# Six per-token inverse roots: spread over the partitions by way of a row in DRAM instead of by TensorE, and the attention pairs of the second layer in another order

## The chip, the core and the metric

The kernel runs on one core of one Trainium2 chip. The core's TensorE (PE, with its weight loads PEld), VectorE (DVE), ScalarE (ACT) and GpSimd (POOL) run their own instruction streams, each in program order; SyncE (SP) here only issues DMAs. The metric is the device time of one execution in microseconds (us): 894.42, the median of three runs (894.36 to 894.44). Lower is better.

## The reference, cut to what matters

```
h = rms_norm(x)                       # n1: 512 tokens x 1024 features
q, k, v, z_a, b, c, u, z_c = h @ w_in
attn = softmax_1(q k) - lam * softmax_2(q k)   # 4 heads, two score maps each
attn = rms_norm(attn @ v) * silu(z_a)          # "an": one norm per head
x = x + rms_norm([attn, conv] @ w_out)         # n2
x = x + sigmoid(x @ w_gate) * rms_norm(p @ w_ple)   # n3
y = gmlp(rms_norm(x))                 # n4; a_w_in -> u, v, z; a_w_out
x = x + rms_norm(y)                   # n5
k, v = rms_norm(x) @ w_kv             # shared by all heads of the next layer
x = x + rms_norm(swa(rms_norm(x), k, v))   # n6; b_w_in, 16 heads, window 128; b_w_out
```

Every `rms_norm` needs, for each token, 1/sqrt(mean of squares + eps).

## The kernel before, in words

Activations lie feature-major: 128 features on the partitions, the 512 tokens along the free axis. All products are float32 made of parts: a tensor is split into a rounded high part (`whi`, `h1h`; ACT copies) and the rest (`wlo`, `h1l`; DVE subtractions), and three matmuls (high x high, high x low, low x high) make one product. Weights arrive as `raw` (128 x 1024, 512 KB) by DMAs of SP, each waiting for its buffer; ACT makes `whi`, DVE makes `wlo`, and the wlo is the last reader of the raw.

The reciprocal roots come out of `cols` as `rstd` with the tokens on the partitions (128 x 4: four blocks of 128 tokens). A feature-major tensor needs the same 512 numbers as a row on every partition. Five kinds of norms (`WIDE` at L42: an, n1, n3, n4, n6) do this in `bcast_wide` (L434): DVE splits rstd into `rh` and `rl`, POOL multiplies each with the identity (`dgh`, `dgl`, 128 x 512), PE multiplies these with a matrix of ones (two matmuls into `bc`), and for an, n1 and n4 ACT copies PSUM to SBUF (`n1rb`, `anrb`, `n4rb`). n1's row is first used by the evictions of q (`ev<-w_in,n1rb`), a head's row by `at<-pv,gsub,anrb` (L207), n4's row by the evictions of u and z, which come after the columns of v (those use n4's columns, not its row).

The order of the program is made when it is built, by a planner (`Flow`, L86 to L150). It holds a model clock for each engine and for each tensor a time at which it is ready; stages are generators that `yield` what they wait for, or a number of model nanoseconds, and the one that is ready first is written next. A change of one model time therefore moves instructions on every engine. On the chip each engine then runs its stream in that order and waits by semaphores.

The second layer's attention takes its work in pairs (pr, b): pr is one half of the heads, b a block of 128 tokens; `ORDER_B` (L38) is their order, `PACE_B` the model time between two units. A pair gives scores `bsc`, transposed probabilities `btr`, `bph`/`bpl`, products `bpv`, the output `y`, its parts `ybh` and `ybl`, and these go into `b_w_out`. `h_tokens` transposes the residual (`ht`, eight groups of four transposes), started at H_START and spaced by PACE_H.

Of the kernel before, what the change touches and what calls it, by code (L numbers as in the profile page):

```python
# [10 lines left out]
F32 = mybir.dt.float32  # L11
F32R = mybir.dt.float32r
AF = mybir.ActivationFunctionType
# [4 lines left out]
P = 128  # L18
T = 512
NT = T // P  # L20
# [14 lines left out]
HB_AT = 7  # L35
POOL_ST6 = False
DENSE_B = (0, 1, 2, 3, 4, 5, 6, 7, 8, 9, 10, 11, 12, 13, 14, 15)
ORDER_B = tuple((pr, b) for pr in range(2) for b in range(4))  # L38
AHEAD_END = 1
H_START = 8000  # L40
LAM_AT = 40000
WIDE = ('an', 'n1', 'n3', 'n4', 'n6')  # L42
LAT = 130.0
KLATE = 3
BANKS = 7

PACE_A, PACE_B, PACE_LN, PACE_H = 4500, 3500, 8000, 4000
WARM = 10


# [35 lines left out]
class Flow:  # L86
# [14 lines left out]
    def at(self, aps):  # L101
        return max((self.ready.get(a.tensor.name, 0.0) + LAT for a in aps), default=0.0)

# [50 lines left out]
def block(ctx: ExitStack, tc: tile.TileContext, xT, pT, w_in, w_out, w_ple, w_gate, a_w_in, a_w_out,  # L154
          w_kv, b_w_in, b_w_out, vecs, rows, bs_rows, gp_rows, csts, w_sT, tri, tabA, tabB, out):
    nc = tc.nc
# [3 lines left out]
    ring = ctx.enter_context(tc.tile_pool(name="ring", bufs=RING))  # L160
    wraw = ctx.enter_context(tc.tile_pool(name="wraw", bufs=WRAW))
    whl = ctx.enter_context(tc.tile_pool(name="whl", bufs=WHL))
    small = ctx.enter_context(tc.tile_pool(name="small", bufs=6))
    psum = ctx.enter_context(tc.tile_pool(name="psum", bufs=8, space=PSUM))
    F = Flow()
    uid = [0]

    def nm(s):
        uid[0] += 1
        return f"{s}_{uid[0]}"  # L170

    def rt(name, dt=F32):
        return ring.tile([P, T], dt, tag="r", name=nm(name))

    def rt2(name):
        return rt(name + "h", F32R), rt(name + "l", F32R)
# [5 lines left out]
    def pst(name):  # L182
        live[0] += name in COUNTED
        return psum.tile([P, T], F32, tag="ps", name=nm(name))
# [10 lines left out]
    def size(a):  # L195
        return math.prod(a.shape[1:])

    def is_ap(*args):
        return [a for a in args if not isinstance(a, (int, float, type(None)))]

    def act(o, a, func, bias=0.0, scale=1.0, accum_out=None, after=0.0):
        nc.scalar.activation(o, a, func, bias=bias, scale=scale, accum_out=accum_out)  # L202
        ex = is_ap(bias, scale, accum_out)
        F.op("act", 80 + 0.84 * size(o) + 93 * len(ex), [o] + is_ap(accum_out), [a] + is_ap(bias, scale), after)

    def stt(o, a, sc, b, op0, op1):
        nc.vector.scalar_tensor_tensor(o, a, sc, b, op0, op1)  # L207
        F.op("dve", 70 + 1.04 * size(o) + 65 * len(is_ap(sc)), [o], [a, b] + is_ap(sc))

    def tt(o, a, b, op, after=0.0):  # L210
        nc.vector.tensor_tensor(o, a, b, op)  # L211
        F.op("dve", 70 + 1.04 * size(o), [o], [a, b], after)

    def ptt(o, a, b, op):
        nc.gpsimd.tensor_tensor(o, a, b, op)  # L215
        F.op("pool", 350 + 260 * size(o) if op == ALU.pow else 100 + 2.4 * size(o), [o], [a, b])
# [17 lines left out]
    def vcopy(o, a):  # L234
        nc.vector.tensor_copy(o, a)
        F.op("dve", 70 + 0.8 * size(o), [o], [a])
# [6 lines left out]
    def mm(o, a, b, start, stop, cost=None):  # L243
        nc.tensor.matmul(o, a, b, start=start, stop=stop)  # L244
        F.op("pe", cost or max(107.0, 2 + b.shape[-1] / 2.4), [o], [a, b])

    def mm3(o, a, b, first, last):
        (ah, al), (bh, bl) = a, b
        mm(o, ah, bh, first, False)
        mm(o, ah, bl, False, False)  # L250
        mm(o, al, bh, False, last)
# [176 lines left out]
    def bcast(r, half=None):  # L428

        o = pst("bc")  # L430
        for t in range(NT) if half is None else (2 * half, 2 * half + 1):
            mm(o[:, t * P:(t + 1) * P], r[:, t:t + 1].to_broadcast([P, P]), ident, True, True, 224)
        return o

    def bcast_wide(r, out):

        rh = small.tile([P, NT], F32R, tag="rh", name=nm("rh"), bufs=2)
        rl = small.tile([P, NT], F32R, tag="rl", name=nm("rl"), bufs=2)
        vcopy(rh, r)
        tt(rl, r, rh.bitcast(F32), ALU.subtract)  # L440
        ds = rt2("dg")
        for d, h in zip(ds, (rh, rl)):
            v = d.rearrange("p (t c) -> p t c", c=P)
            ptt(v, ident.unsqueeze(1).to_broadcast([P, NT, P]), h.bitcast(F32).unsqueeze(2).to_broadcast([P, NT, P]),
                ALU.mult)
        yield list(ds)
        o = pst("bc")
        mm(o, onesr, ds[0], True, False)
        mm(o, onesr, ds[1], False, True)
        out.append(o)  # L450

    def norm(stat, d, name, n=1024, eps=EPS, copy=True, half=None):
        key = name if half is None else (name, half)
        yield lambda: all(stat.n[h] == stat.total for h in ((0, 1) if half is None else (half,)))
        yield stat.acc if half is None else [stat.acc[half]]
        if name == "n1":
            yield 1500
        r = cols(stat.acc, n, eps, half)
        d[name + "c" if half is None else (name + "c", half)] = r
        yield [r]  # L460
        if name in WIDE:
            os = []
            yield from bcast_wide(r, os)
            o = os[0]
        else:
            o = bcast(r, half)
        if copy:
            rb = rt(name + "rb")
            act(rb, o, AF.Copy)
            d[key] = rb  # L470
        else:
            d[key] = o
# [7 lines left out]
    row = const.tile([P, NROW], F32, name="row")  # L480
# [114 lines left out]
    def ev_k2(o, rb, d, key):  # L595
# [8 lines left out]
        if key == 1:  # L604
            yield lambda: KLATE in QB
        second = [rt("kh", F32R), rt("kl", F32R)]
# [95 lines left out]
    def attn_pv(h):  # L702
        yield lambda: all(j in V for j in range(NT))
        yield [a for j in range(NT) for a in V[j]]
        o = pst("pv")
        d = slice(h * P, (h + 1) * P)
        for j in range(NT):
            c = slice(j * P, T)
            ph, pl = A.pop((h, j))
            mm3(o[:, c], [a[:, d] for a in V[j]], (ph[:, c], pl[:, c]), j == 0, j == NT - 1)  # L710
        yield [o]
        sq = rt("asq")
        act(sq, o, AF.Square)
        yield [sq]
        r = cols([sq, sq], P, SUBLN_EPS)
        yield [r]
        if "an" in WIDE:
            os = []
            yield from bcast_wide(r, os)
            bc = os[0]  # L720
        else:
            bc = bcast(r)
        rb = rt("anrb")
        act(rb, bc, AF.Copy)
        yield [rb]
        at = rt("at")
        stt(at, o, gsub, rb, ALU.mult, ALU.mult)
        yield lambda: h in SZA
        tt(at, at, SZA[h], ALU.mult)
        yield [at]  # L730
        yield from gsplit(at, MIX, 3 + h, "ya")
# [45 lines left out]
    os = ko("w_in", 0, h1)  # L777
# [67 lines left out]
    for k in range(2):  # L845
        t = rt("p")
# [100 lines left out]
    def spatial_weights():  # L947
        wst = [rt("wst"), rt("wst")]
        trit = const.tile([P, P], F32, name="trit")
        dma(nc.sync, trit, tri, 64)  # L950
        for i in range(2):
            dma(nc.sync, wst[i], w_sT[i])
        yield wst
        for i in range(2):
            v = wst[i].rearrange("p (g t) -> p g t", t=P)
            tt(v, v, trit.unsqueeze(1).to_broadcast([P, 4, P]), ALU.mult)
        for i in range(4):

            w = rt("ws", F32R)
            v = w.rearrange("p (g s t) -> p g s t", s=2, t=P)  # L960
            src = wst[i // 2][:, i % 2 * 256:i % 2 * 256 + 256].rearrange("p (g t) -> p g t", t=P)
            yield [wst[i // 2]]
            yield from gsplit(src, None, None, "ws", None, (v[:, :, 0], v[:, :, 1]))
            S["w", i] = w
        yield [S["w", i] for i in range(4)]
        yield 4000
        for i in range(2):
            o = pst("rs")
            for j in range(2):
                v = S["w", 2 * i + j].rearrange("p (g s t) -> p g s t", s=2, t=P)  # L970
                for q in range(2):
                    mm(o[:, HALF[j]].rearrange("p (g t) -> p g t", t=P), onesr, v[:, :, q], q == 0, q == 1)
            b = rt("bs")
            dma(nc.sync, b, bs_rows[i])
            rs = rt("rs")
            yield [o]
            act(rs, o, AF.Copy)
            S["rs", i], S["bs", i] = rs, b
# [222 lines left out]
    def swa_master():  # L1201
        for pr, b in ORDER_B:
            yield lambda: pr in KS and all(4 * pr + i in QB for i in range(4))
# [7 lines left out]
    def h_tokens():  # L1211
        yield H_START
        for t in range(NT):
# [57 lines left out]
    for half in range(2):  # L1271
        for j in range(2):
            F.until(lambda: live[0] <= 6)
            os = [pst("b_w_out") for _ in range(2)]
# [102 lines left out]
```

## Time and profile before

| what | value |
|---|---|
| median of three runs | 894.42 us |
| the profiled execution's own time | 894.61 us |
| its span, first to last instruction | 892.9 us |
| granted TensorE clock | 0.999 of full speed |
| TensorE busy | 882.8 us |
| VectorE busy | 637.9 us |
| ScalarE busy | 443.4 us |
| GpSimd busy | 77.8 us |
| DMA, mean rate | 104 GB/s |

Busy shares are means over the whole program: 71% on VectorE is 97% in one stretch of 70 us and far less in others. A wait of TensorE shows in two ways, as idle time before an instruction with the engine that released it, and as a start-to-start distance above the usual one. Matmuls overlap, so their length (0.39 us) is not what one costs.

### The profile page before, as it was taken

To read this page: it belongs to the slowest core of one execution; us is meant where nothing else is said; L and a number is where in the kernel's file an instruction comes from. 1 tells how busy PE (TensorE), PEld (TensorE's weight loads), DVE (VectorE), ACT (ScalarE), POOL (GpSimd) and SP (SyncE) were. 2 spreads that over 40 slices of the span, in tenths; PEclk is the share of its full clock that TensorE was granted. 3 is DMA by queue.
4 is the path that set the end of the run, shared out by engine and by line. 5 is a ranking of instruction groups with operands and counts; after the bars stand their busy time and mean duration, and the time that the engine had idled before them with its cause. 6 is when DMAs were issued, how large, how long until landed. Compare 5 with 4: busy or idle time off the path is not lost.

```text
span 892.9 us, 12066 instructions
## 1 busy us (share of the span) xinstructions
PE 882.8 (99%) x4348; PEld 744.2 (83%) x4348; DVE 637.9 (71%) x1364; ACT 443.4 (50%) x954; POOL 77.8 (9%) x93
## 2 busy tenths in 40 slices
PE   9999999999999999999999999999999999999997
PEld 7888888888888888888888888888899988887785
DVE  6799989653558893338897766683347876989974
ACT  7455554322556544335443333322344646999763
POOL 0100032100000001001000000000000011434100
PEclk9999999999999999999999999999999999999999
DMA  7231222225423242232232222214232158211353
GB/s 263 94 118 48 71 72 71 95 94 189 142 72 116 73 135 104 99 104 81 73 106 88 89 95 95 95 48 141 94 119 72 71 138 223 65 48 48 120 187 118
DMA packets 30443, 93.20 MB, mean 104 GB/s; under 512 B 3888, under 2 KB 4272, under 8 KB 30384
## 3 DMA queue, kind: packets, MB, share of 16 engines
q1 hardware_dynamic: 30384, 92.44, 30.8%
q8 instruction: 34, 0.56, 0.2%
q14 instruction: 25, 0.20, 0.1%
HBM read 85.60 MB, written 2.10 MB: 98 GB/s over the span
## 4 chain that ended last, share of the span: by engine, by line
PE 87%; DVE 9%; issue 1%; ACT 1%; DMA 1%; SPq 0%; DVEq 0%; ACTq 0%
PE a_w_in L244 29%; PE w_in L244 17%; PE a_w_out L244 10%; PE b_w_in L244 6%; PE w_gate L244 5%; PE w_out L244 5%; PE b_w_out L244 4%; PE kv L244 3%; PE sp L244 2%; DVE wlo L211 2%; PE e L244 1%; PE bsc L244 1%; DVE bpl L211 1%; PE sc L244 1%; DVE be L227 1%
## 5 line engine op out<-in xcount | busy, mean ns | idle before, releaser
L211 DVE TENSOR_TENSOR wlo<-raw,whi 128x512 fp32r<-128x512 f32 x280 | 189.1, 701 | 99.4 <-ACT whi L202 95.6
L202 ACT ACTIVATE whi<-raw 128x512 fp32r<-128x512 f32 x280 | 166.4, 623 | 132.5 <-PE a_w_in L244 39.4
L244 PE MATMUL a_w_in<-h2h,whi 128*128 128x512 f32 x256 | 99.8, 390 | 0.0
L244 PE MATMUL a_w_in<-h2l,whi 128*128 128x512 f32 x256 | 99.7, 390 | 0.0
L244 PE MATMUL a_w_in<-h2h,wlo 128*128 128x512 f32 x256 | 99.6, 389 | 0.0
L244 PE MATMUL w_in<-h1h,whi 128*128 128x512 f32 x224 | 89.3, 401 | 0.4 <-ACT h1h L202 0.4
L244 PE MATMUL w_in<-h1h,wlo 128*128 128x512 f32 x224 | 87.0, 390 | 0.0
L244 PE MATMUL w_in<-h1l,whi 128*128 128x512 f32 x224 | 86.9, 390 | 0.0
L215 POOL TENSOR_TENSOR rstd<-var,mhalf 128x4 f32<-128x4 f32 (+2 forms) x15 | 14.7, 981 | 592.9 <-DVE var L222 536.8
L244 PEld LDWEIGHTS a_w_in<-h2h,wlo 128*128 128x128 f32 x256 | 48.1, 188 | 10.2
L244 PEld LDWEIGHTS a_w_in<-h2h,whi 128*128 128x128 f32 x256 | 48.1, 188 | 9.6
L244 PEld LDWEIGHTS a_w_in<-h2l,whi 128*128 128x128 f32 x256 | 48.1, 188 | 9.4
L211 DVE TENSOR_TENSOR sq<-sq,sq 128x512 f32<-128x512 f32 (+1 forms) x44 | 29.3, 666 | 35.5 <-ACT sq L202 33.6
L244 PE MATMUL b_w_in<-hbh,whi 128*128 128x512 f32 x128 | 52.0, 406 | 0.1
L244 PE MATMUL b_w_in<-hbh,wlo 128*128 128x512 f32 x128 | 50.1, 391 | 0.0
L244 PE MATMUL b_w_in<-hbl,whi 128*128 128x512 f32 x128 | 50.0, 391 | 0.0
L244 PE MATMUL a_w_in<-whi,h2h 128*128 128x512 f32 x128 | 50.0, 391 | 0.0
L244 PE MATMUL a_w_in<-whi,h2l 128*128 128x512 f32 x128 | 49.8, 389 | 0.0
L244 PE MATMUL a_w_in<-wlo,h2h 128*128 128x512 f32 x128 | 49.8, 389 | 0.0
L244 PEld LDWEIGHTS w_in<-h1h,whi 128*128 128x128 f32 x224 | 42.4, 190 | 8.8 <-ACT h1h L202 0.7
L244 PEld LDWEIGHTS w_in<-h1h,wlo 128*128 128x128 f32 x224 | 42.0, 188 | 9.0
L244 PEld LDWEIGHTS w_in<-h1l,whi 128*128 128x128 f32 x224 | 42.2, 188 | 7.9
(269 smaller groups left out, 2034.6 us busy)
## 6 DMA issues: line engine op xcount, KB each, us to landing
raw<-in_a_w_in SPq DMA_DIRECT2D x48, 512.0 KB, 3.2
raw<-in_w_in SPq DMA_DIRECT2D x29, 512.0 KB, 3.2
raw<-in_a_w_out SPq DMA_DIRECT2D x16, 512.0 KB, 3.2
raw<-in_b_w_in SPq DMA_DIRECT2D x16, 512.0 KB, 3.8
raw<-in_b_w_out SPq DMA_DIRECT2D x16, 512.0 KB, 3.6
raw<-in_w_out SPq DMA_DIRECT2D x8, 512.0 KB, 3.3
raw<-in_w_gate SPq DMA_DIRECT2D x8, 512.0 KB, 3.2
x<-in_xT SPq DMA_DIRECT2D x8, 256.0 KB, 5.5
```

The lines of the kernel that those rows point to most:

```text
L202: nc.scalar.activation(o, a, func, bias=bias, scale=scale, accum_out=accum_out)
L211: nc.vector.tensor_tensor(o, a, b, op)
L215: nc.gpsimd.tensor_tensor(o, a, b, op)
L227: nc.vector.tensor_tensor_reduce(o, a, b, 1.0, s0, ALU.add, ALU.max, mx)
L244: nc.tensor.matmul(o, a, b, start=start, stop=stop)
```

## The change

For n1, n4 and the four heads' norms a new function writes the 128 x 4 inverse roots into a row of DRAM (512 single numbers, `row`), and a second DMA reads that row for all 128 partitions (`n1rb`, `anrb`, `n4rb`, 128 x 512). Both are issued by SP. n3 and n6 stay as they were. The planner reckons 2600 ns for each of the two DMAs. The pairs (1,0) and (1,1) now stand before (0,3); `h_tokens` starts at once and with closer spacing; the matmuls `rs` of the spatial weights start 4000 model ns later. The function and its place of call:

```
-ORDER_B = tuple((pr, b) for pr in range(2) for b in range(4))
+ORDER_B = ((0, 0), (0, 1), (0, 2), (1, 0), (1, 1), (0, 3), (1, 2), (1, 3))
-H_START = 8000
+H_START = 0
+DMA_ROW = 2600
-PACE_A, PACE_B, PACE_LN, PACE_H = 4500, 3500, 8000, 4000
+PACE_A, PACE_B, PACE_LN, PACE_H = 4500, 3500, 8000, 3500
+    dram = ctx.enter_context(tc.tile_pool(name="dram", bufs=4, space=bass.MemoryType.DRAM))
+    def bcast_dma(r, name):
+
+        row_ = dram.tile([NT, P], F32, tag="row", name=nm("row"))
+        nc.sync.dma_start(row_.rearrange("t p -> p t"), r)
+        F.ready[row_.tensor.name] = F.at([r]) + DMA_ROW
+        yield [row_]
+        rb = rt(name + "rb")
+        nc.sync.dma_start(rb, row_.rearrange("t p -> (t p)").unsqueeze(0).to_broadcast([P, T]))
+        F.ready[rb.tensor.name] = F.at([row_]) + DMA_ROW
+        return rb
@@ norm
+        if name in ('n1', 'n4', ''):
+            d[key] = yield from bcast_dma(r, name)
+            return
@@ attn_pv
-        if "an" in WIDE:
-            os = []
-            yield from bcast_wide(r, os)
-            bc = os[0]
-        else:
-            bc = bcast(r)
-        rb = rt("anrb")
-        act(rb, bc, AF.Copy)
+        rb = yield from bcast_dma(r, "an")
@@ spatial_weights
-        yield 4000
+        yield 8000
```

On SP's stream at the first norm, before: six loads of weights one after the other (the numbers in the names are only numbers of tiles).

```order
22 L239 DMA raw_195<-in_w_in 128x1024
23 L239 DMA raw_292<-in_w_in 128x1024
24 L239 DMA raw_300<-in_w_in 128x1024
25 L239 DMA raw_326<-in_w_in 128x1024
26 L239 DMA raw_402<-in_w_in 128x1024
27 L239 DMA raw_469<-in_w_in 128x1024
```

The same place of SP's stream after the change:

```order
22 L241 DMA raw_197<-in_w_in 128x1024
23 L241 DMA raw_294<-in_w_in 128x1024
24 L241 DMA raw_302<-in_w_in 128x1024
25 L241 DMA raw_328<-in_w_in 128x1024
26 L457 DMA row_339<-rstd_323 128x4x1
27 L461 DMA n1rb_360<-row_339 128x512
28 L241 DMA raw_392<-in_w_in 128x1024
29 L241 DMA raw_465<-in_w_in 128x1024
```

The two new DMAs stand behind the loads of rows 22 to 25 and ahead of the next one, which waits behind them.

On VectorE at the first head's norm, before: the work on scores (ISA rows, `s`), on transposed probabilities (`ptl`) and on the gate (`zas`) ahead of `at`, the first use of the head's row.

```order
197 L220 TENSOR_SCALAR s_1076<-s_1076,rs_1125 128x128
198 L207 SCALAR_TENSOR_TENSOR s_1076<-s_1078,rs_1125,s_1076 128x128
199 L211 TENSOR_TENSOR ptl_888<-tr_1084,pth_887 128x128
200 L211 TENSOR_TENSOR ptl_890<-tr_1084,pth_889 128x128
201 L211 TENSOR_TENSOR ptl_892<-tr_1084,pth_891 128x128
202 L207 SCALAR_TENSOR_TENSOR zas_1156<-zat_1101,za_1099 128x512
203 L227 ISA s_1158,nmx_1145<-sc_1147,tbA_87 128x256
204 L227 ISA nmx_1145 128x1
205 L227 ISA s_1160,nmx_1145<-sc_1150,tbA_87 128x256
206 L227 ISA nmx_1145 128x1
207 L220 TENSOR_SCALAR neg_1162<-nmx_1145 128x2
208 L207 SCALAR_TENSOR_TENSOR at_1169<-pv_907,gsub,anrb_1113 128x512
```

The same place of VectorE's stream after the change:

```order
189 L213 TENSOR_TENSOR wlo_1020<-raw_852,whi_1019 128x512
190 L233 RECIPROCAL rs_1112<-ssum_1056 128x2
191 L213 TENSOR_TENSOR rs_1112<-rs_1112,nlam 128x1
192 L222 TENSOR_SCALAR s_1066<-s_1066,rs_1112 128x128
193 L209 SCALAR_TENSOR_TENSOR s_1066<-s_1068,rs_1112,s_1066 128x128
194 L209 SCALAR_TENSOR_TENSOR at_1129<-pv_915,gsub,anrb_1101 128x512
195 L209 SCALAR_TENSOR_TENSOR zas_1139<-zat_1081,za_1079 128x512
```

`at` now follows directly on the `s` of 128 x 128; the three ptl, a zas and the score work that stood between come behind it.

On TensorE at the end of the second layer's attention, before: `b_w_out` products, which need the pairs' `ybh` and `ybl`, with `bpv` products of later pairs between them.

```order
3956 L244 MATMUL b_w_out_8071<-whi_8073,ybh_8155 128x512
3957 L244 MATMUL b_w_out_8071<-wlo_8074,ybh_8155 128x512
3958 L244 MATMUL b_w_out_8071<-whi_8073,ybl_8156 128x512
3959 L244 MATMUL bpv_8213<-bph_8086,vz_6598 128x512
3960 L244 MATMUL bpv_8213<-bpl_8087,vz_6598 128x512
3961 L244 MATMUL bpv_8213<-bph_8136,vz_6602 128x512
3962 L244 MATMUL bpv_8213<-bpl_8137,vz_6602 128x512
3963 L244 MATMUL b_w_out_8072<-whi_8073,ybh_8191 128x512
3964 L244 MATMUL b_w_out_8072<-wlo_8074,ybh_8191 128x512
3965 L244 MATMUL b_w_out_8072<-whi_8073,ybl_8192 128x512
```

The same products after the change, with the transposes of the residual (`ht`) between them:

```order
3956 L246 MATMUL b_w_out_8066<-whi_8068,ybh_8124 128x512
3957 L246 MATMUL b_w_out_8066<-wlo_8069,ybh_8124 128x512
3958 L246 MATMUL b_w_out_8066<-whi_8068,ybl_8125 128x512
3959 L256 MATMUL ht_8193<-ident,y_5707 128x128
3960 L256 MATMUL ht_8193<-ident,y_5781 128x128
3961 L256 MATMUL ht_8193<-ident,y_5855 128x128
3962 L256 MATMUL ht_8193<-ident,y_5929 128x128
3963 L246 MATMUL b_w_out_8067<-whi_8068,ybh_8131 128x512
3964 L246 MATMUL b_w_out_8067<-wlo_8069,ybh_8131 128x512
3965 L246 MATMUL b_w_out_8067<-whi_8068,ybl_8132 128x512
```

They stand at the same row numbers, although twelve matmuls (the `bc` pairs) are gone further ahead: twelve matmuls of other work, eight `bpv` products and four `ht` transposes, have moved ahead of them.

## Rows read from the trace of the kernel before

**Rows 1.** The page, busy time: us, share of the span, instructions

```profile
PE 882.8 (99%) x4348; PEld 744.2 (83%) x4348; DVE 637.9 (71%) x1364; ACT 443.4 (50%) x954; POOL 77.8 (9%) x93
```

**Rows 2.** The page, chain that ended last, by engine

```profile
PE 87%; DVE 9%; issue 1%; ACT 1%; DMA 1%; SPq 0%; DVEq 0%; ACTq 0%
```

**Rows 3.** Waits of TensorE: us in total, times, longest

```profile
PE b_w_out L244 <- DVE ybl L211: 0.8, 2, 0.5
...
PE tr L254 <- DVE s L207: 0.4, 1, 0.4
PE rs L244 <- ACT gv L202: 0.2, 1, 0.2
```

**Rows 4.** Windows: stretch, TensorE, weight loads, VectorE, ScalarE, GpSimd, clock, DMA, GB/s

```profile
40.00:70.00 30.00, 30.00 (x142) 24.73 (x141) 29.16 (x80) 14.77 (x39) 0.00 (x0) 1.00 0.26 88
70.00:110.00 40.00, 39.65 (x202) 33.23 (x201) 38.78 (x113) 21.30 (x62) 3.06 (x3) 1.00 0.19 67
110.00:150.00 40.00, 40.00 (x206) 33.79 (x205) 36.33 (x103) 20.84 (x62) 8.11 (x7) 1.00 0.22 75
```

**Rows 5.** Timeline of TensorE at n1's products: start us, us, instruction

```profile
30.08 0.39 PE L244 MATMUL bc<-dgh,onesr 128*128 128x512 f32 x1
...
30.54 0.40 PE L244 MATMUL w_in<-h1h,whi 128*128 128x512 f32 x1
```

**Rows 6.** Timeline, GpSimd and VectorE at n1

```profile
24.91 1.41 POOL L215 TENSOR_TENSOR rstd<-var,mhalf 128x4 f32<-128x4 f32 x1 [23.62 <-DVE var L222]
...
31.36 0.69 DVE L207 SCALAR_TENSOR_TENSOR ev<-w_in,n1rb 128x512 f32<-128x512 f32 x1 [0.65 <-ACT n1rb L202]
```

**Rows 7.** Timeline of SyncE near n1; then DMA issues, 24 to 40 us

```profile
26.06 0.33 SPq L239 DMA_DIRECT2D raw<-in_w_in  x1
...
raw<-in_w_in SPq DMA_DIRECT2D x3, 512.0 KB, 4.5
```

**Rows 8.** The page, DMA issues: KB each, us from issue to landing

```profile
raw<-in_w_in SPq DMA_DIRECT2D x29, 512.0 KB, 3.2
...
out<-y SPq DMA_DIRECT2D x8, 256.0 KB, 2.3
...
p<-in_pT SPq DMA_DIRECT2D x2, 256.0 KB, 6.5
```

**Rows 9.** Timeline of VectorE, 94 to 100 us, first and last

```profile
94.25 0.48 DVE L211 TENSOR_TENSOR ptl<-tr,pth 128x128 fp32r<-128x128 f32 x2
...
99.97 0.68 DVE L211 TENSOR_TENSOR ptl<-tr,pth 128x128 fp32r<-128x128 f32 x3
```

**Rows 10.** Timeline, VectorE and GpSimd, 90 us and 134 us

```profile
90.51 0.16 DVE L235 CAST rh<-rstd 128x4 fp32r<-128x4 f32 x1
...
90.79 0.16 DVE L231 RECIPROCAL rs<-ssum 128x2 f32<-128x2 f32 x1
...
90.83 1.04 POOL L215 TENSOR_TENSOR dgh<-ident,rh 128x512 fp32r<-128x512 f32 x1 [5.23 <-DVE rh L235]
...
90.98 0.90 DVE L211 TENSOR_TENSOR rs<-rs,nlam 128x1 f32<-128x1 f32 x1
91.80 1.27 DVE L220 TENSOR_SCALAR s<-s,rs 128x384 f32<-128x384 f32 x1
93.11 0.62 DVE L207 SCALAR_TENSOR_TENSOR s<-s,rs,s 128x384 f32<-128x384 f32 x1
...
134.62 0.16 DVE L211 TENSOR_TENSOR rs<-rs,nlam 128x1 f32<-128x1 f32 x1
...
135.15 0.62 DVE L207 SCALAR_TENSOR_TENSOR s<-s,rs,s 128x384 f32<-128x384 f32 x1
```

**Rows 11.** Timeline of TensorE, 108 us

```profile
108.03 0.44 PE L254 MATMUL tr<-ident,s 128*128 128x128 f32 x2 [0.35 <-DVE s L207]
```

**Rows 12.** Timeline of TensorE, 845 us

```profile
845.05 0.50 PE L244 MATMUL b_w_out<-whi,ybl 128*128 128x512 f32 x1 [0.51 <-DVE ybl L211]
```

## The prediction

> **What bounds the kernel now.** Read the busy times first: TensorE is busy for 882.8 us, VectorE for 637.9 [rows 1]. So the program is nearly one long row of matmuls, and a microsecond is won either by taking matmuls out or by closing a wait of TensorE. The chain of waits says where that isn't all: 9% of the path runs through VectorE [rows 2]. The list of TensorE's waits gives the places: transposes that wait for VectorE's `s` (0.4), output products that wait for `ybl` (0.8), the `rs` products (0.2) [rows 3]. Last the windows, because a mean hides stages: from 40 to 110 us VectorE works 29.16 of 30 and 38.78 of 40 us, so in the first attention it is as full as TensorE; from 110 to 150 us it has 3.7 us to spare [rows 4]. What is late on VectorE before 40 us is still late at 108 us, where a transpose waits 0.35 us for it [rows 11]. This stretch decides the sign.
>
> **Removed from TensorE.** Two matmuls for each of six norms. From the first of n1's pair to the next weight product it is 0.46 us (30.54 − 30.08) [rows 5], not the 0.39 us that each lasts, since they overlap. Six pairs: 2.76 us, of which two (n1 and the first head), 0.92 us, stand ahead of 108 us, and four, 1.84 us, behind. TensorE is busy around all of them, so I count them whole. The four later pairs are a gain unless something waits; the first two count only if TensorE, not VectorE, leads at 108 us.
>
> **n1's row comes later.** Before, `rstd` ends at 24.91 + 1.41 = 26.32 us and the first eviction starts at 31.36 [rows 6]: 5.0 us for casts, identity products, matmuls and copy. Now two DMAs in a row, on SP behind three loads. The last of these is issued at 26.06, and such a load takes 4.5 us here (the median of three) [rows 7], to about 30.5. The write of the row is issued at about 26.4. No DMA of this kind, with single numbers going to DRAM, is in the trace. If it shared the DMA engines at once with the loads and cost little, the chain would be done in time: 26.4 + 2.3 + 0.1 + 2.3 = 31.1, with the 2.3 us of an output store for each leg [rows 8], a delay of 0. At the other end each leg takes the 6.5 us of the `p` loads [rows 8]: 26.4 + 13.1 = 39.5, a delay of 8. I take the case between: its packets queue behind the loads' packets and land at 31.0, the second DMA is issued 0.1 later and takes 2.3: 33.4, a delay of 2.1 us. Behind it wait the evictions, q and k, the scores, and with them all of VectorE. The next load on SP stands behind the second DMA too; it waits for its buffer in any case, and I count nothing for it.
>
> **The first head's row.** It is used by `at`. On SP the row's write now stands behind a weight load that waits for a `wlo` on VectorE. From the end of that `wlo` to `at` the new order has the instructions that the trace runs from 94.25 to 99.97, less the `wlo` itself: 5.72 − 0.60 = 5.1 us [rows 9] (the length of a step is taken from start to start). The path needs 0.33 us for the load's issue, some 3.4 for the row behind the load's 3.2 [rows 7, 8], and 2.3 for the second DMA: 6.0. VectorE stands for 0.9 us (0 to 8.2, with the same two ends). For the other three heads more VectorE work or VectorE's idle time (3.7 us from 110 to 150) covers it, and I count nothing; if the DMAs are slow this cover goes first. n4's row is needed only for u and z, long after: nothing.
>
> **Given back on VectorE.** The two casts of the first head's norm, 90.51 to 90.79, are 0.28 us [rows 10]; n1's lie in idle time. More comes from POOL. While POOL makes `dgh` and `dgl` (1.04 us each), VectorE's tiny `rs` lasts 0.90 us and the following `s` 1.27 us; from the start of `rs` to the second `s` it is 93.11 − 90.98 = 2.13 us, where the same three steps take 135.15 − 134.62 = 0.53 us without POOL [rows 10]. That is 1.6 us in the full stretch, and these products are gone. Together 1.9 us. If the lengthening had another cause, it stays: bound 0.3 to 1.9.
>
> **At 108 us.** VectorE leads there, so TensorE's time moves with it: 2.1 + 0.9 − 1.9 = +1.1 us, its own two pairs (−0.92) being swallowed. Part of it is paid earlier, at the first transposes near 55 us, but it is the same debt.
>
> **Moved work.** `rs` moves behind n4's place, so its wait of 0.2 us goes. At the end of the second attention twelve matmuls, eight `bpv` and four `ht`, now stand ahead of the products that wait for `ybl`. Eight at half a pair are 1.8 us of cover against waits of 0.8 us in two places, the longest 0.51 [rows 3, 12]. After a wait a matmul takes about 0.50 instead of 0.39 us [rows 12, 5], so the three waits are worth 0.8 + 0.2 + 3 × 0.1 = 1.3 us. I take it all; the other end is as much again the wrong way, since pairs in another order may leave VectorE or ScalarE late at a new place. The `ht` transposes are eight groups of four in both orders; their place among other matmuls costs nothing, and the copies (ACT) and n's casts lie beside matmuls.
>
> **Sum.** +1.1 − 1.84 − 1.3 = −2.0 us. The profiled execution took 894.61 (span 892.9 and some 1.7 around it), so 892.6; it ran 0.2 above the median, so **892.4**.
>
> **Rivals.**
>
> 1. *The DMAs are in time.* No delay at n1 or the first head. Then VectorE gains 1.9 at 108 us and TensorE leads: it gets its 0.92, and the wait of 0.35 with its restart 0.1 goes: −1.4 − 1.84 − 1.3 = −4.5, or 889.9. For it: the load ahead of n1's row is issued 0.3 us before, and a small write need not wait for a large read. Against: the three loads are one queue, and theirs took 4.5 us instead of 3.2 [rows 7, 8].
>
> 2. *The delays eat the gain.* Delay at n1 plus delay at the first head of about 5 us (each chain of two DMAs some 1 us longer than I take): 5.1 − 1.9 = +3.2 at 108 us, − 3.1 behind it: 894.5, no change. What can be told from no change here is 0.2%, 1.8 us; so the two delays must sum to between about 3.2 and 6.8 us.
>
> 3. *Slower: the write of 512 single numbers is slow.* Each row is 128 partitions of four numbers that go to places 512 bytes apart, and the program waits for that write twice in its fullest stretch. With 6.5 us for the write and 2.3 for the read: n1's row at 26.4 + 6.5 + 0.1 + 2.3 = 35.3, a delay of 3.9; the first head 0.3 + 8.9 − 5.1 = 4.1. At 108 us +8.0 − 1.9 = 6.1, later −3.1: +3.0, or 897.4, more if further heads lose their cover. It decides from a sum of the delays near 7 us, which is about 5.9 us for the write. For it: nothing in the trace of this kind is known to be quick. Against: 2 KB is very little. The Trainium skill, page "DMA: Bandwidth & Descriptors", section "Rules for kernel authors", speaks for this rival: a pattern whose last dimension isn't contiguous becomes one descriptor per element, and a plain DMA that transposes by a rearranged pattern is 19 times slower than the hardware's transpose. No run here shows that yet; taken at its word for so small a transfer, it makes the slow case, not mine.
>
> **Chances.** The forecast, a sum of delays of 1 to 3.2 us: 0.36, its own range 890.8 to 892.7. Rival 1: 0.18. Rival 2: 0.27. Rival 3: 0.19. Faster is the first two, 0.54; same 0.27; slower 0.19. The range goes from rival 1's time to just under rival 3's, 889.8 to 897.0: below it lies almost nothing, above it half of rival 3 and what the moved pairs may do wrong.
>
> **What would show it.** The list of DMA issues gives row and rb to landing: under 2.5 us each with the first eviction at or before 31.4 is rival 1; 31.0 and 33.4 for n1 is mine; a row of 6 us is rival 3. In the timeline of VectorE no `rs` of 0.9 us and no `s` of 1.27 us should stand near 91 us; if one does, the 1.6 us was not POOL's. The waits of TensorE should show new ones at the scores near 45 us or the transposes near 55 us of about 2 us, and none on `ybl` or `rs`. Wrong altogether would be a span in which the first 110 us are as long as before and the time has moved in the second attention: then the order of the pairs counted, which I take for a small term.

## The result and the profile after

The changed kernel takes 916.86 us (median of 4 runs, 915.13 to 917.38), 2.45% longer than before (ratio 1.0245, 95% interval 1.0232 to 1.0257). The forecast was 892.4, with a range up to 897.0. Its profiled execution took 917.11 us, 22.5 more than the 894.61 of before.

Busy times, clock and chain of the page, after:

```profile
span 915.3 us, 12020 instructions
...
PE 888.1 (97%) x4336; PEld 746.8 (82%) x4336; DVE 632.8 (69%) x1352; ACT 439.6 (48%) x948; POOL 64.0 (7%) x81
...
PEclk9989989999999999999999999999999999999999
...
PE 72%; DVE 4%; DMA 2%; ACT 1%; issue 1%; SPq 0%; POOL 0%; DVEq 0%; ACTq 0%; POOLq 0%
```

Beside [rows 1, 2]: TensorE does 12 matmuls less and is busy 5.3 us longer, which a count of instructions can't give; a look at the clock can. The chain can't be set beside the one before: its shares sum to 80%, since it was followed back only to 177 us. What it holds of the rows is the fourth head's: its write, 10.6 us, and its read, 4.4.

The new DMAs on the page of issues (KB each, us from issue to landing), after; before, no DMA went to or from such a row:

```profile
anrb<-row SPq DMA_DIRECT2D x4, 256.0 KB, 4.5
n1rb<-row SPq DMA_DIRECT2D x1, 256.0 KB, 3.7
n4rb<-row SPq DMA_DIRECT2D x1, 256.0 KB, 5.9
row<-rstd SPq DMA_DIRECT2D x6, 2.0 KB, 8.6
```

The 2 KB write takes 8.6 us (7.7 to 10.6 over the six), longer than anything in [rows 8], the 512 KB loads of weights among it. The waits of VectorE, SyncE and TensorE (us in total, times, longest), after:

```profile
DVE at L209 <- DMA anrb<-row: 29.0, 4, 9.0
...
DVE ev L209 <- DMA n1rb<-row: 8.8, 1, 8.8
```

```profile
SPq L461 <- DMA row<-rstd: 48.4, 6, 10.2
```

```profile
PE sc L246 <- DVE kl L213: 5.6, 2, 4.9
PE sc L246 <- DVE at L209: 4.5, 1, 4.5
PE st L246 <- ACT asq L204: 4.0, 2, 2.6
PE pv L246 <- DVE ptl L213: 1.3, 1, 1.3
...
PE b_w_out L246 <- DVE ybl L213: 1.0, 1, 1.0
```

SyncE waits six times for the row to land before it can issue the second DMA, VectorE waits five times for the second, and TensorE stops one step later, at what VectorE makes next. None of these lines of TensorE names a row's DMA: the cause stands two waits up the chain. No wait in TensorE's whole list ends at a `wlo` or a load of weights either, so SyncE's stand did not starve TensorE of weights here. The two steps that matter most, n1's on SyncE and VectorE and the first head's on VectorE, after:

```profile
26.29 0.39 SPq L457 DMA_DIRECT2D row<-rstd  x1
35.57 0.34 SPq L461 DMA_DIRECT2D n1rb<-row  x1
...
39.30 1.89 DVE L209 SCALAR_TENSOR_TENSOR ev<-w_in,n1rb 128x512 f32<-128x512 f32 x3 [8.77 <-DMA n1rb<-row]
...
114.10 0.75 DVE L209 SCALAR_TENSOR_TENSOR at<-pv,gsub,anrb 128x512 f32<-128x512 f32 x1 [7.36 <-DMA anrb<-row]
```

Against [rows 3], the waits on `rs` and on `s` are gone; the one on `ybl` isn't.

The first long hole in TensorE's timeline (start us, us, instruction, idle before and its releaser), after:

```profile
51.70 0.47 PE L246 MATMUL sc<-kl,qs 128*128 128x128 f32 x1 [4.91 <-DVE kl L213]
51.97 0.42 PE L246 MATMUL sc<-kh,qs 128*128 128x128 f32 x1
53.12 0.48 PE L246 MATMUL sc<-kl,qs 128*128 128x128 f32 x1 [0.73 <-DVE kl L213]
53.40 0.73 PE L246 MATMUL w_in<-whi,h1h 128*128 128x512 f32 x1
53.93 0.63 PE L246 MATMUL w_in<-wlo,h1h 128*128 128x512 f32 x1
54.36 0.63 PE L246 MATMUL w_in<-whi,h1l 128*128 128x512 f32 x1
...
56.49 0.40 PE L246 MATMUL w_in<-wlo,h1h 128*128 128x512 f32 x1
56.73 0.40 PE L246 MATMUL w_in<-whi,h1l 128*128 128x512 f32 x1
```

Behind the hole the same matmuls start 0.43 us apart, and only from 56.49 on 0.23 to 0.24 as before. The windows show why (the eighth value is the granted clock), after:

```profile
45.00:50.00 5.00, 1.00 (x4) 0.40 (x3) 4.88 (x8) 3.17 (x6) 0.00 (x0) 0.97 0.01 4
50.00:55.00 5.00, 2.57 (x7) 2.09 (x8) 4.86 (x9) 0.57 (x1) 0.00 (x0) 0.50 0.07 11
55.00:60.00 5.00, 5.00 (x21) 4.02 (x21) 4.79 (x15) 3.34 (x10) 0.00 (x0) 0.85 0.27 99
...
115.00:120.00 5.00, 4.47 (x11) 3.38 (x12) 4.97 (x17) 2.42 (x8) 0.00 (x0) 0.50 0.13 44
```

Behind this hole and the first head's, from 50 to 55 us and from 115 to 120 us, the clock stands at 0.50, its lower level, 1.2 instead of 2.4 GHz.

**Where the 22.5 us are.** Taking each start-to-start distance above the usual one (0.23 us for 512 columns), from 20 us to the last `b_w_out` product: the holes of over 0.36 us sum to 21.5 us after and 3.5 before; the smaller excesses, nearly all at the lower clock, to 8.3 and 1.0. That is 18.0 + 7.3 = 25.3 us lost, less the six pairs of matmuls, 2.8: 22.5, the difference measured. n1 has 7.2 of the holes, the first head 5.6, the other three heads 6.7, 19.5 in all; the small waits that went (at 108 us and at `rs`) and the second attention take 1.5 off.

### The profile page after: what moved, and what is told of

Its sections match the earlier page's. It is cut to its first block, busy times and chain, and to the rows that moved or that the text cites. A ratio compares the mean times of both kernels' runs of the same rounds, so it can differ in the third digit from the quotient of the medians.

```text
span 915.3 us, 12020 instructions
## 1 busy us (share of the span) xinstructions
PE 888.1 (97%) x4336; PEld 746.8 (82%) x4336; DVE 632.8 (69%) x1352; ACT 439.6 (48%) x948; POOL 64.0 (7%) x81
## 4 chain that ended last, share of the span: by engine, by line
PE 72%; DVE 4%; DMA 2%; ACT 1%; issue 1%; SPq 0%; POOL 0%; DVEq 0%; ACTq 0%; POOLq 0%
PE a_w_in L246 29%; PE a_w_out L246 10%; PE b_w_in L246 7%; PE w_gate L246 5%; PE w_out L246 5%; PE b_w_out L246 5%; PE w_in L246 3%; PE kv L246 3%; PE sp L246 2%; PE e L246 1%; DMA row<-rstd 1%; DVE be L229 1%; PE bpv L246 1%; PE btr L256 1%; PE bsc L246 1%; DMA qh<-ql 1%
## 5 line engine op out<-in xcount | busy, mean ns | idle before, releaser
L246 PE MATMUL w_in<-h1h,wlo 128*128 128x512 f32 x224 | 88.9, 399 | 0.1
L213 DVE TENSOR_TENSOR sq<-sq,sq 128x512 f32<-128x512 f32 (+1 forms) x44 | 29.3, 666 | 35.6 <-ACT sq L204 33.7
```

## The experiments

Theory: the write of single numbers lands late, and VectorE and SyncE, in program order, stand for it; the lower clock adds to each hole; the order of the pairs matters little. Rivals: the order; the trip through DRAM as such; SyncE's stand, starving the weights.

**The order alone (e1).** All six norms by products again, the rest of the change kept.

```
-        if name in ('n1', 'n4', ''):
-            d[key] = yield from bcast_dma(r, name)
-            return
-        rb = yield from bcast_dma(r, "an")
+        os = []
+        yield from bcast_wide(r, os)
+        rb = rt("anrb")
+        act(rb, os[0], AF.Copy)
```

> All six norms go by products with ones as before; only the pairs' order, the start and pace of the ht transposes and the later rs products are of the change. Theory (the row in DRAM lands 8 to 10 us after its issue and VectorE and SyncE wait for it in order; the rest of the change is small): 892.5 to 895.5 us, with the waits on ybl (0.8 us before) changed by no more than 1 us. Rival (the new order of the pairs costs much of the 22 us): 900 us or more.

Measured: 894.15 us, ratio 0.9994 (0.9985 to 1.0003). The order is not the loss, nor a gain that this can tell.

```profile
PE b_w_out L246 <- DVE ybl L213: 1.0, 1, 1.0
PE tr L256 <- DVE s L209: 0.3, 1, 0.3
```

These are two of e1's waits of TensorE. `rs` waits no more; `ybl` waits once for 1.0 us instead of twice for 0.8 in all.

**n1 and n4 alone (e2).** As e1, but n1 and n4 keep the row.

> n1 and n4 go by the row in DRAM, the four heads by products with ones as before; the rest is as in the changed kernel. Theory: n1's row comes at about 39.3 us instead of 31.4, TensorE stops for 7 us at the scores near 45 to 53 us and runs at the lower clock for some us after it: 901 to 904 us, so about a third of the loss is n1's and two thirds are the heads'. Rival (n1's delay is caught up before 110 us, all of the loss is the heads'): 894 to 897 us.

Measured: 901.51 us, 1.0074 (1.0056 to 1.0091). So about 7 us are n1's (n4's row is waited for by nobody) and about 15 the heads'. TensorE's largest waits in e2 are n1's, as in the changed kernel:

```profile
PE sc L246 <- DVE kl L213: 5.6, 2, 4.9
PE sc L246 <- ACT kh L204: 1.2, 1, 1.2
```

**A planner that knows (e3).** `F.at([r]) + 8500` and `F.at([row_]) + 4500` in place of `DMA_ROW` twice.

> As the changed kernel, but the planner reckons 8500 ns for the write and 4500 ns for the read in place of 2600 each, so it writes the use of each head's row later in VectorE's stream. Theory (VectorE standing at the head's first use is what costs): the 29 us that VectorE waits for the four heads' rows fall to under 8, the time to 900 to 908 us; n1's wait stays, there is no other work to put ahead of it. Rival (SyncE, which waits for the write before it issues the next weights, starves the weights): the time stays above 912 us and the waits move to the raw loads.

Measured: 902.94 us, 1.0096 (1.0078 to 1.0114), 14 us less than the changed kernel, with DMAs as slow (a row lands after 9.6 us). VectorE's wait for the heads' rows fell from 29.0 to 1.3 us, since other work now stands ahead of `at`. Its waits for rows in e3:

```profile
DVE ev L209 <- DMA n1rb<-row: 4.7, 1, 4.7
...
DVE at L209 <- DMA anrb<-row: 1.3, 1, 1.3
```

SyncE's stand at the rows fell too, from 48.4 to 23.3 us, so this run doesn't part the two by itself. But no hole of TensorE in e3 goes back to a load: its largest wait stands at a `wlo` of VectorE, which works without a break from the eviction at 41 us until it comes to this `wlo` at 59 us. It is n1's delay at another place:

```profile
PE w_in L246 <- DVE wlo L213: 7.8, 1, 7.8
```

**The write by itself (e4).** The kernel before, with twelve small writes for which nothing waits, 15 to 21 us apart in a quiet stage, each issued right behind a load of weights.

```
+            nc.sync.dma_start(a.rearrange("t p -> p t"), src)   # pa: a [4,128] in DRAM
+            nc.sync.dma_start(b, src)                           # pb: b [128,4]
+            nc.sync.dma_start(c, ident[0:NT, :])                # pc: c [4,128]
+            nc.sync.dma_start(e[:, :, 0], src)                  # pe: e [128,4,128]
+            nc.sync.dma_start(f, vec[:, 4:5])                   # pf: f [128,1]
+            nc.sync.dma_start(pq[:, 0::2], src)                 # pq in SBUF
```

> The kernel before with twelve small writes that nobody waits for, in its long quiet stage (400 to 600 us), six kinds twice: pa 512 single numbers into a 2 KB row, order t p (as the change writes it); pb the same numbers as 128 pieces of 16 bytes; pc 4 pieces of 512 bytes; pe 512 single numbers, each 512 bytes from the next; pf 128 single numbers in a row; pq 512 single numbers into SBUF. Issue to landing: if single numbers next to each other in DRAM are the trouble (engines write parts of the same line): pa 6 to 9 us, pe under 4, pb and pf between, pc and pq about 2. If the count of pieces is: pa, pe and pq alike, 6 to 9 us, pb and pf about 3, pc 2. If any small write to DRAM is slow: all but pq above 5 us. Its time is 894 to 896 us in all cases.

Measured: 894.22 us. The page of issues has landings for three kinds:

```profile
pb<-vec SPq DMA_DIRECT2D x2, 2.0 KB, 3.2
...
pe<-vec SPq DMA_DIRECT2D x2, 2.0 KB, 3.3
...
pq<-vec SPq DMA_DIRECT2D x2, 2.0 KB, 3.9
```

For all six the trace holds the single steps by which the DMA engines tell of a landing. Issue to the last step, first and second probe (us):

```
pa  512 single numbers, next to each other in DRAM   9.1   9.8
pf  128 single numbers, next to each other in DRAM   8.2   8.8
pe  512 single numbers, 512 bytes apart in DRAM      3.3   3.3
pb  128 pieces of 16 bytes, next to each other       3.4   3.1
pc  4 pieces of 512 bytes                            2.9   2.6
pq  512 single numbers into SBUF                     4.8   3.1
```

Neither the count of pieces (pe and pq have 512) nor small writes to DRAM as such (pb) are slow, but single numbers side by side. pb and pf, both put in the middle, came out on opposite sides: pf is nearly as slow as pa with a quarter of the pieces. The packets aren't what lasts: pa's were over 2.9 and 2.5 us after the issue, while the sixteen steps came from 4.8 to 9.1 us, and from 6.3 to 9.8. What the memory does in between, no run shows.

**Pieces of 16 bytes (e5).** The row lies as rstd does, the second DMA reads it into `rp`, and ACT puts the copy in order.

```
-        row_ = dram.tile([NT, P], F32, tag="row", name=nm("row"))
-        nc.sync.dma_start(row_.rearrange("t p -> p t"), r)
+        row_ = dram.tile([P, NT], F32, tag="row", name=nm("row"))
+        nc.sync.dma_start(row_, r)
...
+        act(rb.rearrange("p (t c) -> p t c", c=P), rp.rearrange("p (c t) -> p t c", t=NT), AF.Copy)
```

> The changed kernel, but the row in DRAM lies partition by partition (128 pieces of 16 bytes next to each other instead of 512 single numbers), and one ACT copy puts the numbers in order after the second DMA (0.6 us each). The planner's 2600 + 2600 ns stay. Theory (single numbers beside each other are slow to write, 9.1 and 9.8 us in the probe against 3.1 and 3.4 for pieces of 16 bytes): row lands after about 3.3 us where nothing is queued ahead; n1 is some 3 us late instead of 7.9, VectorE's 29 us of waits for the heads' rows fall to 8 to 14; 900 to 906 us. Rival (the trip through DRAM by two DMAs costs it, whatever the layout): above 911 us.

Measured: 895.0 us, 1.0004 (0.9995 to 1.0013), outside both ranges. The layout, with the copy that it needs, takes back 22 us, more than I expected; the trip through DRAM as such isn't what made the loss, though it isn't free either (e9). n1's eviction begins at 35.41 us, some 4 late instead of 7.9; TensorE waits 1.9 us at the scores, against 6.4 in the changed kernel, and 1.9 at a `tr`. e5's DMA issues, and VectorE's waits for the rows (the copies stand for them):

```profile
row<-rstd SPq DMA_DIRECT2D x6, 2.0 KB, 2.6
```

```profile
DVE ev L209 <- ACT n1rb L204: 4.5, 1, 4.5
...
DVE at L209 <- ACT anrb L204: 3.2, 1, 3.2
```

Three of the four heads' waits are gone, since 2.6 us fall within their cover where 8.6 didn't.

**n1 by products, pieces, planner told (e6).** e5 with 3400 and 4600 ns for the planner and `'n4'` alone in the list of norms.

> n1 by products again; the heads and n4 by the row of 16-byte pieces and an ACT copy, and the planner reckons 3400 + 4600 ns for the two DMAs. Theory: no wait of VectorE or TensorE for a row is left, five pairs of matmuls are gone (5 x 0.46 = 2.3 us), and VectorE is not held up by the identity products: 890.5 to 892.5 us, faster than both kernels. Rival (VectorE's order, with the heads' last steps put later, makes TensorE wait elsewhere in the first attention): 893.5 to 896 us.

Measured: 890.04 us, 0.9951 (0.9939 to 0.9964): below the expected range and faster than both kernels. No wait of TensorE or VectorE for a row from DRAM is left. TensorE's list in e6, whole but for the warm-up:

```profile
PE b_w_out L246 <- DVE ybl L213: 1.0, 1, 1.0
PE bsc L246 <- DMA qh<-ql: 0.9, 1, 0.9
PE w_in L246 <- ACT h1h L204: 0.6, 1, 0.6
```

**n1 by products, single numbers, planner told (e7).** e3 with the same list as e6.

> As e3 (planner told 8500 + 4500 ns, single numbers), but n1 by products. Theory (all that was left in e3 is n1's delay): 892 to 894.5 us, the heads' slow rows hidden behind other work. Rival (SyncE, standing 8 us at each row, makes the weights late): 896 us or more, with waits of TensorE that end at wlo in 100 to 200 us.

Measured: 895.54 us, 1.0014 (1.0005 to 1.0023). A miss: a slow write isn't hidden for nothing even when the planner knows. But the waits are not the rival's either: three heads' rows are late by 4.8 us in all (a row lands after 9.4 us here, more than the 8.5 told), and TensorE waits 2.8 us at `s`, behind that. e6, with the pieces and their times told, is 5.5 us faster. e7's two waits:

```profile
PE tr L256 <- DVE s L209: 2.8, 1, 2.8
```

```profile
DVE at L209 <- DMA anrb<-row: 4.8, 3, 4.0
```

**The hole filled (e8).** e2 with 25 matmuls, whose result isn't used, ahead of the first scores.

```
+        if (h, b) == (0, 0):
+            fill = pst("fill")
+            for _ in range(25):
+                nc.tensor.matmul(fill, onesr, h1[0][0], start=True, stop=True)
```

> As e2 (n1 and n4 by the row, heads by products), with 25 matmuls of 128 x 512 put on TensorE ahead of the first scores; their result is not used. In e2 TensorE idles from 45 to 53 us and its clock stands at 0.5 to 0.6 of full speed until about 59 us, with matmuls 0.43 us apart instead of 0.23. The filling takes about 5.7 us, the length of the hole. Theory (the lower clock comes from the idle time and costs some 2 us beside it): about 2 us less than e2, 898.5 to 900.3 us. Rival (the clock falls anyway, or fill costs what it saves): 901 us or more.

Measured: 900.01 us, 1.0063 (1.0049 to 1.0076), 1.5 less than e2, as expected. The two intervals overlap, so the times alone don't settle it; the clock does. The windows of e2 and of e8 over the same stretch:

```profile
50.00:55.00 5.00, 2.31 (x6) 1.88 (x7) 4.88 (x8) 0.31 (x1) 0.00 (x0) 0.50 0.00 0
55.00:60.00 5.00, 5.00 (x15) 3.92 (x14) 4.78 (x16) 3.59 (x10) 0.00 (x0) 0.60 0.32 110
```

```profile
50.00:55.00 5.00, 3.47 (x17) 2.61 (x16) 4.90 (x8) 0.00 (x0) 0.00 (x0) 1.00 0.00 0
55.00:60.00 5.00, 5.00 (x26) 4.21 (x24) 4.76 (x16) 3.92 (x10) 0.00 (x0) 1.00 0.31 107
```

With TensorE kept busy the clock stays at 1.00, and 26 matmuls instead of 15 run from 55 to 60 us.

**All six in pieces, planner told (e9).** e5 with 3400 and 4600 ns.

> All six rows in 16-byte pieces with the ACT copy, as in e5, and the planner told 3400 + 4600 ns, as in e6: the fourth corner beside the changed kernel (single numbers, not told), e3 (single numbers, told) and e5 (pieces, not told). Theory (layout and planner's times each take away their own part, and what is left is n1's delay of about 4 us): 892 to 894.5 us, no wait of VectorE for a head's row, one of 4 to 5 us for n1's. Rival (n1's delay costs nothing once the planner knows it): 889 to 890.5 us, as e6 or better.

Measured: 894.9 us, 1.0002 (0.9987 to 1.0017); 0.4 above my range. No head's row is waited for, as expected; of n1's wait of 4 to 5 us only 0.3 is left, since a `wlo` now stands ahead of it on VectorE, but the eviction still begins at 36.20 us, 4.8 late, and TensorE waits for VectorE further on, at `tr` (2.4) and `wlo` (1.3). Beside e6, n1's row costs about 5 us even in pieces. Beside e5 (1.0004), telling the planner brought nothing that can be told.

**The old order (e10).** e6 with the pairs' order and the three paces of before.

> As e6 (n1 by products, the rest by rows in pieces, told), with the pairs' order, H_START, PACE_H and the start of rs of the kernel before. Theory (the order is worth nothing that can be measured, as e1 showed): within 0.8 us of e6, 889.5 to 891 us. Rival (the order is worth a microsecond or more together with the rows): 891.2 us or more.

Measured: 891.41 us, 0.9970 (0.9957 to 0.9983). It falls into the rival's range, 1.4 above e6. But the intervals of e6 and e10, each against the kernel before, overlap (e6 ends at 0.9964), and the spans of the two profiled executions differ by 0.5 us (888.5 and 889.0); whether the order is worth a microsecond beside the rows stays open.

## Why the prediction was wrong, point by point

*What bounds it* was right in part. VectorE stood for n1's row and the first head's, and TensorE behind it. But the first head's hole in TensorE, 110 to 115 us, lies at the end of the full stretch, and for the other three heads' rows VectorE stood up to 143, 166 and 198 us, where the prediction took its other work and idle time for cover.

*Removed matmuls*: no run takes the six pairs out alone; e6 and e1 differ by 4.1 us with five pairs gone, 2.3 by the rows, with the wait at 108 us and POOL's products beside them.

*n1's row* is the step that failed first. I took 31.0 us for the row's landing, by the loads queued ahead of it, and 33.4 for the second DMA: a delay of 2.1. The row was issued at 26.29 and landed 9.3 us later at 35.6, the second DMA took 3.7, and the eviction began at 39.30 instead of 31.36: 7.9 late. The queue was a true wait but not the long one: the row's packets were over at 30.2 us; its landing came 5.4 later. I had given the write almost nothing of its own, 0.5 us behind the loads' end at 30.5; its 9.3 us instead of 4.6 and the read's 3.7 instead of 2.3 are the missing 6. (33.4 less 31.36 is 2.0, not 2.1, and a sum of delays of 1 us gives 890.4 by that sum, not 890.8; neither bears on the outcome.)

*The first head's row* failed in the same term, the write that was to land 0.2 us behind a load: 0.9 us taken, 7.36 measured. The cover was right: 5.1 us taken from the `wlo`'s end to `at`, 5.4 in the trace. *The other heads*: nothing taken; they made 21.6 of VectorE's 29.0 us of waits. Their cover was counted against a chain of 6 us; it took 13 to 15.

*The bounds* failed too. The upper end, 6.5 us for a leg, was the slowest transfer in sight, and six writes took 7.7 to 10.6. A kind of transfer with no row in the trace isn't bounded by those of other kinds.

*Given back on VectorE*: right. The same three steps without POOL, after:

```profile
99.63 0.16 DVE L213 TENSOR_TENSOR rs<-rs,nlam 128x1 f32<-128x1 f32 x1
99.70 0.42 DVE L222 TENSOR_SCALAR s<-s,rs 128x384 f32<-128x384 f32 x1
100.16 0.62 DVE L209 SCALAR_TENSOR_TENSOR s<-s,rs,s 128x384 f32<-128x384 f32 x1
```

From `rs` to the second `s` it is 0.53 us, against 2.13 in [rows 10]: the 1.6 us came back, where VectorE had to stand anyway.

*Moved work*: the `rs` wait went as forecast. The `ybl` waits did not: 1.0 us in the changed kernel and in e1, against 0.8 of [rows 3]. Twelve matmuls more ahead of the products didn't help, since VectorE's own work had moved as well (after, three `y<-bpv`, 2.1 us, stand right ahead of the late `ybl`, where before they came one at a time); the 1.0 us that I gave it was not there.

*The missing term* is the clock. The sum had holes priced at their length; behind four of them the granted clock was 0.50, for 3.4 to 6.8 us. That is 7.3 of the 25.3 us lost, and in e8, with the hole filled, the clock did not fall.

*The rivals*: the third had the mechanism, the write of single numbers, but at 0.19 and 897.4 us it had too little chance and 19 us too little price, for want of the clock, the other heads and the true landing (6.5 us taken, 7.7 to 10.6 measured). Its reason was not the one either: it named places 512 bytes apart, and pe, with just that, is quick; slow are numbers that lie next to each other, as those of neighbouring partitions do in this row. The Trainium skill, page "DMA: Bandwidth & Descriptors", section "Rules for kernel authors", which I set beside it, warned of the right pattern; the reason it gives, one descriptor per element, doesn't decide here, as pe has as many as pa and lands in 3.3 us.

## What to carry to other kernels

Before a step is sent through DRAM, look at how its pieces lie there, not at its bytes: a write of 2 KB took 9 us as neighbouring single numbers and 3 us in pieces of 16 bytes. Price a wait on an engine whose stream is full by its whole length, plus what TensorE loses at its lower clock behind the hole. And give a planner the measured latency: the same slow transfers cost 14 us less when other work was written ahead of their use (e3), while a row that nothing can cover, such as n1's, is better kept on the engines (e6 against e9).

## What the runs showed of the hardware

- In e4, 512 single numbers side by side in DRAM land 9.1 and 9.8 us after their issue, 128 of them 8.2 and 8.8, but 512 bytes apart 3.3; the packets of the 512 are over within 3 us.
- The sixteen steps of one such DMA's landing come over several microseconds (n1's row: from 3.1 to 9.3 us after the issue; over 1.8 to 7.6 us in the six), those of a 16-byte layout (e5) within 0.2 to 1.6.
- In the changed kernel TensorE was busy for 1.00 us of the 5 from 45 to 50 us; from 50 to 55 us its granted clock was 0.50, and from 53.93 to 56.49 us matmuls of 512 columns were 0.43 us apart, then 0.23 to 0.24. In e8, with the hole filled, the clock stayed at 1.00.
